# Two modulation tiles move from around the second branch's values to the end of attention

## The chip, the core and the metric

The kernel runs on one core of one Trainium2 chip. The metric is the device time of one execution in microseconds (us). Names in the text: TensorE is PE in the profile (its weight loads are PEld), VectorE is DVE, ScalarE is ACT, GpSimd is POOL, SyncE is SP. A line such as L203 is a line of the kernel before.

## What is computed

One decoder layer over 512 tokens of 1024 channels, in float32. A conditioning vector `c` gives six modulation vectors; two attention branches share one input projection; a gated MLP follows.

```python
mod = c @ w_ada + b_ada
sh1, sc1, gt1, sh2, sc2, gt2 = [m[:, None, :] for m in jnp.split(mod, N_MOD, axis=-1)]
u = x * (1.0 + sc1) + sh1
proj = u @ w_in
q_a, k_a, v_a, f_a, q_b, k_b, v_b, g_a, g_b = jnp.split(proj, _split_points(), axis=-1)
...
merged = jax.nn.sigmoid(g_a) * (y_fox @ w_fox_proj) + jax.nn.sigmoid(g_b) * (y_sb @ w_sb_proj)
attn_out = merged @ w_o
x = _layer_norm(DEEPNORM_ALPHA * x + (1.0 + gt1) * attn_out, ln1_g, ln1_b)
u2 = x * (1.0 + sc2) + sh2
```

Branch A is forgetting attention (softmax with a decay, "FoX"), branch B is stick-breaking attention. `sh2` and `sc2`, two of the six modulation vectors, are needed only after the first layer norm.

## The kernel before

**Products.** Every float32 weight is split into a rounded high half and the rest (`wh` by ScalarE at L183, `wl` by VectorE at L93), and each product is three matmuls, high by high, high by low and low by high (L134 to L136 for projections, L456 to L458 for the values).

**Items.** Weights come as tiles of 128x1024 (512 KB) through one list, `items`, in the order in which the code adds them. SyncE issues the loads in that order (L157). While attention runs, `depth` is 4: the load of an item is issued only after VectorE has read the item four places ahead of it (`paced`). The buffer `raw` has five slots, `wh` and `wl` three each. A projection that begins processes its own item and the two behind it.

**The stream.** The attention stage interleaves a list of TensorE work, `stream`, with the heads. The list holds the projections of queries and keys by pair of heads ("q4" is the tile of pair 4's queries; pairs 1 to 3 are of the stick-breaking branch, 4 to 7 of FoX), the values of a branch (`add_values`, four items, `vgroup`), the gates (`add_gate`) and the projections of the heads' outputs (`bproj`, whose weights are `in_wp`). `FILL` says how many matmuls stand between the steps of a head: scores (`stage_a`, L481 and L482), transposes of the probabilities (`stage_b`, L540), product with the values (`stage_c`, L558). PSUM has eight banks, given out in turn; a transpose needs three.

**Modulation tiles.** The 24 tiles of `in_wa` numbered 0 to 23 are items too. `add_ada` puts the next one into the list behind a projection. Numbers 8 to 23 are summed on VectorE against `c` by `mod_sum` (L203, one pass over 128x1024 with an accumulator, then DVE_READ_ACCUMULATOR) and feed `modr`, which L850 reads once all are there; they give `sh2` and `sc2`. Of the 27 places at which `add_ada` is called, 24 are used, in order; what is not placed by then is added behind the last projection.

**Order on the engines.** SyncE's order is that of the code. On the other engines a scheduler decides it when the kernel is built. The values of FoX are evacuated by `v_evac`: per bank two high halves on ScalarE (L90, `vv`) and two low halves on VectorE (L93, `vv`).

Of the kernel before, what the change touches and what calls it, by code (L numbers as in the profile page):

```python
# [51 lines left out]
def layer_kernel(ctx: ExitStack, tc: tile.TileContext, out, xT, x, cT, crow, wa0, wa1, bcol, bgt, w1, wct, wv, bf,  # L52
# [89 lines left out]
    def add_item(src, proc, cols=1024):  # L142
        items.append([src, proc, cols, None, None])
        return len(items) - 1
# [49 lines left out]
    for e in range(2):  # L194
        c = slice(e * 512, (e + 1) * 512)
# [383 lines left out]
    def ada_proc(n):  # L579
        def f(r):  # L580
            if 8 <= n < 24:
                mod_sum(2 + (n - 8) // 8, n % 8, r, slice(0, D), 0)
                return
            g, q = n // 4, n % 4
            if q == 0:
                ada_st[g] = z(F32, "ac2")
                V.tensor_scalar_mul(ada_st[g], r[:, 0:512], cTs[:, 0:1])  # L587
            acc = ada_st[g]
            for e in range(2):
                k = 2 * q + e  # L590
                if k > 0:
                    a = V.scalar_tensor_tensor(acc, r[:, e * 512 : (e + 1) * 512], cTs[:, k : k + 1], acc, ALU.mult, ALU.add)
                    state["read"] = a
        return f
# [24 lines left out]
    def gate_after(br, j):  # L619
        def f(ps):  # L620
            sg[(br, j)] = z(F32, "sg")
            S.activation(sg[(br, j)], ps, AF.Sigmoid)
        return f
# [42 lines left out]
    skip = [0]  # L666

    def add_ada(n=1):
        for _ in range(n):
            if skip[0]:  # L670
                skip[0] -= 1
            elif adas[0] < 24:
                add_item(wa1[adas[0]], ada_proc(adas[0]))
                adas[0] += 1
                if adas[0] in (4, 8):
                    stream.append((ada_split, (adas[0] // 4 - 1, len(items) - 1)))
                    sums.append([len(stream) + 3, adas[0] // 4 - 1])
# [4 lines left out]
    def add_proj(n, after):  # L682
        stream.append((proj, (add_item(wct[TILES.index(n)], split_proc), after)))
        flush_sum(len(stream))
# [12 lines left out]
    def add_pair(p):  # L697
        br, pr = seq[p]
        for c, ev in (("q", q_evac), ("k", k_evac)):
            if (c, p) in TILES:  # L700
                add_proj((c, p), lambda ps, ev=ev: ev(br, pr, ps))
                marks[(p, c)] = len(stream)
                add_ada(p > 1)

    def add_values(br, ada):
        for j in range(4):
            late = br == 0 and j == 2
            n = add_item(wv[br, j], v_proc if late else split_proc)
            if late:
                vfi.append(n)  # L710
            stream.append((vgroup, (br, j, n)))
            add_ada(ada)

    def add_gate(br, j):
        add_proj(("sb" if br == 1 else "fox", j), gate_after(br, j))
        add_ada()

    gb = list(range(NG, KT))
    add_pair(1)
    add_values(1, 1)  # L720
    marks["v1"] = len(stream)
    add_pair(2)
    add_gate(1, gb.pop(0))
    add_pair(3)
    add_gate(1, gb.pop(0))
    add_pair(4)
    marks["vf"] = len(stream) + 2
    add_values(0, 0)
    add_gate(1, gb.pop(0))
    add_pair(5)  # L730
    marks["y1"] = len(stream)
# [260 lines left out]
    for n in range(2 * FT):  # L992
        wui.append(add_item(wup[n], split_proc))
        if n in GTILES:
            k = GTILES.index(n)
            wai[(10, 28)[k // 4]] = add_item(wa1[(28, 24)[k // 4] + k % 4], ada_proc((28, 24)[k // 4] + k % 4))
        if n in (15, 19):
            p = (15, 19).index(n)
# [8 lines left out]
        if n in (28, 31, 32, 35):  # L1007
            k = (28, 31, 32, 35).index(n)
# [364 lines left out]
```

## Time and profile before

| | |
|---|---|
| median of 3 runs | 746.93 us (746.73 to 747.04) |
| the profiled execution's own time | 746.97 us |
| its span | 745.2 us |
| busy share of the span | PE 98%, PEld 82%, DVE 82%, ACT 52%, POOL 11% |
| the chain that ended last, by engine | PE 96%, DVE 2%, DMA 1%, ACT 1% |
| granted TensorE clock | 0.997 |

The span runs from the first instruction to the last of one execution; the run's own time is 1.8 us more. Of matmuls the end is modelled, so small gaps between them are read from their starts. "idle before <-X" in a timeline row is how long the engine stood ahead of that row, and what released it.

### The profile page before, as it was taken

How to read it: one execution, taken by the hardware profiler on the slowest of the kernel's cores; microseconds unless marked ns; L12 is line 12 of the kernel's file. 1: busy time of each engine (PE TensorE's matmuls, PEld its weight loads, DVE VectorE, ACT ScalarE, POOL GpSimd, SP SyncE). 2: the span in 40 equal slices, each digit the busy share in tenths (PEclk: the TensorE clock that was granted, in tenths of full speed). 3: DMA queues.
4: the chain of work that ended last, by engine and by line, in shares of the span. 5: the costliest groups of instructions: out<-in, count | busy, mean ns of one | idle time of the engine just before them, and what ended most of it. 6: DMA issues, size and time to landing. Idle time of an engine off the chain costs nothing.

```text
span 745.2 us, 9875 instructions
## 1 busy us (share of the span) xinstructions
PE 733.0 (98%) x3476; PEld 609.2 (82%) x3476; DVE 607.8 (82%) x1019; ACT 389.6 (52%) x683; POOL 83.0 (11%) x130
## 2 busy tenths in 40 slices
PE   8999999999999999999999999999999999999995
PEld 5878888887888888888889888888888888888885
DVE  6869799888788795884577899988877797779995
ACT  4566475694875654443055455444454453347550
POOL 1026223354000000000000000000001001000010
PEclk9999999999999999999999999999999999999998
DMA  9943545413413240652052788578788867647633
GB/s 324 404 177 113 170 170 181 158 58 114 171 58 114 72 155 28 211 191 84 1 211 87 206 289 241 201 214 247 246 303 226 252 198 216 211 156 227 223 88 85
DMA packets 45220, 131.95 MB, mean 177 GB/s; under 512 B 5905, under 2 KB 6417, under 8 KB 45170
## 3 DMA queue, kind: packets, MB, share of 16 engines
q1 hardware_dynamic: 38610, 113.66, 44.6%
q0 software_dynamic: 3536, 9.24, 6.6%
q10 hardware_dynamic: 3024, 8.41, 3.1%
q8 instruction: 27, 0.44, 0.2%
q14 instruction: 23, 0.19, 0.1%
HBM read 118.38 MB, written 12.85 MB: 176 GB/s over the span
## 4 chain that ended last, share of the span: by engine, by line
PE 96%; DVE 2%; DMA 1%; ACT 1%; issue 0%; DVEq 0%
PE ps L134 19%; PE ps L135 19%; PE ps L136 19%; PE ps L307 5%; PE ps L1102 5%; PE ps L1104 5%; PE ps L1103 5%; PE ps L558 3%; PE ps L540 2%; PE ps L900 2%; PE ps L899 2%; PE ps L901 2%; PE ps L457 2%; PE ps L458 2%; PE ps L456 2%; PE ps L481 1%
## 5 line engine op out<-in xcount | busy, mean ns | idle before, releaser
L183 ACT ACTIVATE wh<-raw 128x1024 fp32r<-128x1024 f32 (+1 forms) x105 | 109.4, 1044 | 111.0 <-PE ps L135 44.2
L93 DVE TENSOR_TENSOR wl<-raw,wh 128x1024 fp32r<-128x1024 f32 (+2 forms) x114 | 135.2, 1187 | 33.8 <-ACT wh L183 33.3
L134 PE MATMUL ps<-u2h,wh 128*128 128x512 f32 (+1 forms) x376 | 141.5, 376 | 0.0
L135 PE MATMUL ps<-u2l,wh 128*128 128x512 f32 (+1 forms) x376 | 141.2, 376 | 0.0
L136 PE MATMUL ps<-u2h,wl 128*128 128x512 f32 (+1 forms) x376 | 141.2, 376 | 0.0
L134 PEld LDWEIGHTS ps<-u2h,wh 128*128 128x128 f32 x376 | 70.8, 188 | 13.1 <-issue 0.3
L135 PEld LDWEIGHTS ps<-u2l,wh 128*128 128x128 f32 x376 | 70.8, 188 | 12.8
L136 PEld LDWEIGHTS ps<-u2h,wl 128*128 128x128 f32 x376 | 70.8, 188 | 12.7
L134 PE MATMUL ps<-uh,wh 128*128 128x512 f32 x200 | 79.4, 397 | 0.0
L135 PE MATMUL ps<-ul,wh 128*128 128x512 f32 x200 | 78.3, 391 | 0.0
L136 PE MATMUL ps<-uh,wl 128*128 128x512 f32 x200 | 78.2, 391 | 0.0
L1152 ACT ACTIVATE cv<-ps,cw 128x512 f32<-128x512 f32 x44 | 34.0, 773 | 43.8 <-PE ps L136 37.7
L1153 DVE SCALAR_TENSOR_TENSOR cv<-ps,cw,cv 128x511 f32<-128x511 f32 x44 | 32.8, 745 | 17.2 <-ACT cv L1152 17.1
L136 PEld LDWEIGHTS ps<-uh,wl 128*128 128x128 f32 x200 | 37.6, 188 | 8.2
L520 POOL TENSOR_TENSOR pt<-pt,om 128x127 f32<-128x127 f32 (+3 forms) x32 | 43.1, 1357 | 7.8 <-DVE om L519 7.8
L134 PEld LDWEIGHTS ps<-uh,wh 128*128 128x128 f32 x200 | 37.6, 188 | 7.3
L135 PEld LDWEIGHTS ps<-ul,wh 128*128 128x128 f32 x200 | 37.6, 188 | 7.2
L162 POOL DMA_DIRECT2D raw<-in_wdp x10 | 9.1, 909 | 248.6 <-DVE ac L587 184.2
L1154 DVE SCALAR_TENSOR_TENSOR cv<-ps,cw,cv 128x510 f32<-128x510 f32 x44 | 32.7, 742 | 0.3
L1160 ACT ACTIVATE cv<-cv 128x512 f32<-128x512 f32 x22 | 13.9, 630 | 33.4 <-DVE cv L1154 33.4
L519 DVE TENSOR_TENSOR_SCAN om<-om,dg 128x127 f32<-128x127 f32 (+3 forms) x32 | 29.6, 981 | 0.5 <-ACT om L514 0.5
L1104 PE MATMUL ps<-wh,hv 128*128 128x512 f32 x72 | 28.0, 389 | 0.0
(235 smaller groups left out, 1583.0 us busy)
## 6 DMA issues: line engine op xcount, KB each, us to landing
raw<-in_wup SPq DMA_DIRECT2D x44, 512.0 KB, 5.7
raw<-in_wa SPq DMA_DIRECT2D x32, 512.0 KB, 4.2
raw<-in_wct SPq DMA_DIRECT2D x25, 512.0 KB, 3.5
raw<-in_wdp SPq DMA_DIRECT2D x20, 512.0 KB, 6.0
wa<-in_wa SPq DMA_DIRECT2D x14, 512.0 KB, 8.3
raw<-in_wdp SPq DMA_DIRECT2D x22, 256.0 KB, 4.5
raw<-t SPq DMA_DIRECT2D x22, 256.0 KB, 3.9
raw<-in_wdp POOLq DMA_DIRECT2D x10, 512.0 KB, 7.8
```

The costliest lines, as they stand in the source:

```text
L93: state["read"] = V.tensor_tensor(o, i, fl(hi), ALU.subtract)
L134: PE.matmul(ps, wh, ah, start=first, stop=False)
L135: PE.matmul(ps, wh, al, start=False, stop=False)
L136: return PE.matmul(ps, wl, ah, start=False, stop=last)
L183: state["hi"] = S.activation(h[:, 0:cols], r[:, 0:cols], AF.Copy)
L307: PE.matmul(grp[g], w, u, start=j == 0 and n == 0, stop=j == KT - 1 and n == (1 if g == 7 else 2))
L520: G.tensor_tensor(pt[b][:, s : e - 1], pt[b][:, s : e - 1], om[:, s + 1 : e], ALU.mult)
L1102: PE.matmul(ps, ah, bh, start=first, stop=False, skip_group_check=onto)
L1103: PE.matmul(ps, ah, bl, start=False, stop=False, skip_group_check=onto)
L1104: return PE.matmul(ps, al, bh, start=False, stop=last, skip_group_check=onto)
L1152: S.activation(t, ps, AF.Identity, bias=cw[:, n, 3:4], scale=cw[:, n, 2:3])
L1153: V.scalar_tensor_tensor(t[:, 1:], ps[:, 0:511], cw[:, n, 1:2], t[:, 1:], ALU.mult, ALU.add)
```

## The change

```diff
@@ add_pair
             if (c, p) in TILES:
                 add_proj((c, p), lambda ps, ev=ev: ev(br, pr, ps))
                 marks[(p, c)] = len(stream)
-                add_ada(p > 1)
+                add_ada(p > 1 and (p, c) != (4, "k"))
@@
     add_pair(4)
     marks["vf"] = len(stream) + 2
     add_values(0, 0)
+    skip[0] = 1
     add_gate(1, gb.pop(0))
     add_pair(5)
```

`skip` stands in the kernel before as well, always 0: while it is above 0, a call of `add_ada` adds nothing and counts it down. So two places at which a tile was added, behind the keys of pair 4 (tile 11) and behind the gate that follows the FoX values (tile 12), stay empty. Each later tile comes two places later: 11 behind q5, 12 behind k5, 13 behind q6, 14 behind k6, and so on. The last two, 22 and 23, come behind the gates 5 and 6 of FoX, at two places that were not used. No operation is added or removed. SyncE issues as many loads, two of them later.

**VectorE at the evacuation of the FoX values.** `vv` are the values, `yf` and `yl` a finished head, `raw` with `modr` a modulation tile, `wl` a weight's low half, L503 the first softmax. Before:

```order
L203 SCALAR_TENSOR_TENSOR raw_1972,modr<-raw_1972,cbc 128x1024
L565 TENSOR_TENSOR yf_1672<-ps_1799,ytmp_1808 64x512
L93 TENSOR_TENSOR yl_1812<-yf_1672,yh_1811 128x512
L93 TENSOR_TENSOR vv_1818<-ps_1600,vv_1818 128x2x128
L93 TENSOR_TENSOR vv_1821<-ps_1600,vv_1821 128x2x128
L93 TENSOR_TENSOR vv_1830<-ps_1601,vv_1830 128x2x128
L203 SCALAR_TENSOR_TENSOR raw_2061,modr<-raw_2061,cbc 128x1024
L93 TENSOR_TENSOR vv_1833<-ps_1601,vv_1833 128x2x128
L93 TENSOR_TENSOR vv_1842<-ps_1602,vv_1842 128x2x128
L503 TENSOR_REDUCE sm_1888<-ps_1870 128x1
L503 TENSOR_REDUCE sm_1888<-ps_1872 128x1
L93 TENSOR_TENSOR vv_1845<-ps_1602,vv_1845 128x2x128
```

and after the change:

```order
L203 SCALAR_TENSOR_TENSOR raw_1967,modr<-raw_1967,cbc 128x1024
L93 TENSOR_TENSOR wl_1793<-raw_1737,wh_1792 128x1024
L565 TENSOR_TENSOR yf_1669<-ps_1799,ytmp_1808 64x512
L93 TENSOR_TENSOR yl_1812<-yf_1669,yh_1811 128x512
L93 TENSOR_TENSOR vv_1818<-ps_1603,vv_1818 128x2x128
L93 TENSOR_TENSOR vv_1821<-ps_1603,vv_1821 128x2x128
L93 TENSOR_TENSOR vv_1830<-ps_1604,vv_1830 128x2x128
L93 TENSOR_TENSOR vv_1833<-ps_1604,vv_1833 128x2x128
L93 TENSOR_TENSOR vv_1842<-ps_1605,vv_1842 128x2x128
L503 TENSOR_REDUCE sm_1888<-ps_1870 128x1
L503 TENSOR_REDUCE sm_1888<-ps_1872 128x1
L93 TENSOR_TENSOR vv_1845<-ps_1605,vv_1845 128x2x128
```

The tile between the third and the fourth `vv` is gone from there, and the tile ahead of `yf` (now number 12, before 14) stands ahead of the split of q5. Further up, the tile ahead of the last four stick-breaking scans (number 13 before) is gone too.

**VectorE ahead of the second FoX head's softmax.** `wl_2065` and `wl_2059` are q6, `wl_2146` and `wl_2140` are k6. Before:

```order
L93 TENSOR_TENSOR wl_2065<-raw_2059,wh_2064 128x1024
L203 SCALAR_TENSOR_TENSOR raw_2142,modr<-raw_2142,cbc 128x1024
L565 TENSOR_TENSOR yf_1994<-ps_1985,ytmp_1995 64x512
L93 TENSOR_TENSOR wl_2146<-raw_2140,wh_2145 128x1024
L503 TENSOR_REDUCE sm_2034<-ps_2016 128x1
```

and after, with `wl_1970` the split of k5, which stood between the softmax's reductions before:

```order
L93 TENSOR_TENSOR wl_1970<-raw_1914,wh_1969 128x1024
L93 TENSOR_TENSOR wl_2059<-raw_2053,wh_2058 128x1024
L565 TENSOR_TENSOR yf_1988<-ps_1979,ytmp_1989 64x512
L203 SCALAR_TENSOR_TENSOR raw_2136,modr<-raw_2136,cbc 128x1024
L93 TENSOR_TENSOR wl_2140<-raw_2134,wh_2139 128x1024
L503 TENSOR_REDUCE sm_2028<-ps_2010 128x1
```

The tile now stands directly ahead of k6's split, and k5's split has come down to this place. On TensorE, whose order is the same but for this, the second L481 of the third FoX head's scores now stands ahead of the first L482.

**VectorE and SyncE at the end of attention.** On VectorE before, with `wl_3177` gate 5, `wl_3213` gate 6, `raw_3125` and `raw_3165` the tiles 2 and 3 of `in_wo`:

```order
L93 TENSOR_TENSOR wl_3177<-raw_3163,wh_3176 128x1024
L639 TENSOR_TENSOR raw_3165<-raw_3165,gt_1207 128x1024
L93 TENSOR_TENSOR wol_3170<-raw_3125,woh_3168 128x512
L93 TENSOR_TENSOR wl_3213<-raw_3199,wh_3212 128x1024
L93 TENSOR_TENSOR wol_3171<-raw_3125,woh_3169 128x512
```

and after (`wl_3171` gate 5, `raw_3159` modulation tile 22, `raw_3193` and `raw_3119` tiles 3 and 2 of `in_wo`):

```order
L93 TENSOR_TENSOR wl_3171<-raw_3157,wh_3170 128x1024
L203 SCALAR_TENSOR_TENSOR raw_3159,modr<-raw_3159,cbc 128x1024
L639 TENSOR_TENSOR raw_3193<-raw_3193,gt_1207 128x1024
L93 TENSOR_TENSOR wol_3164<-raw_3119,woh_3162 128x512
L633 TENSOR_TENSOR sg_3000<-ps_3156,sg_3000 128x512
L93 TENSOR_TENSOR wol_3165<-raw_3119,woh_3163 128x512
```

Tile 22 stands between gate 5 and `in_wo` 3, and gate 6's split is no longer among these rows. The loads on SyncE from gate 5 on, after the change (`raw_3195` is gate 6, four places behind `in_wo` 2, which stands just ahead of these rows; `raw_3253` is tile 23):

```order
L157 DMA raw_3157<-in_wct 128x1024
L157 DMA raw_3159<-in_wa 128x1024
L157 DMA raw_3193<-in_wo 128x1024
L157 DMA raw_3195<-in_wct 128x1024
L157 DMA raw_3253<-in_wa 128x1024
L157 DMA raw_3255<-in_wp 128x1024
```

Before, no `in_wa` stood among them, and gate 6 was the second load behind gate 5.

## Prediction

> **What bounds the kernel now.** First the page's totals:
>
> ```profile
> span 745.2 us, 9875 instructions
> PE 733.0 (98%) x3476; PEld 609.2 (82%) x3476; DVE 607.8 (82%) x1019; ACT 389.6 (52%) x683; POOL 83.0 (11%) x130
> ```
>
> TensorE sets the time; the change takes no matmul away, so it can only change the time in which TensorE stands. Next the waits of TensorE alone, of which this is the longest inside attention:
>
> ```profile
> PE ps L540 <- DVE vv L93: 1.2, 2, 0.7
> ```
>
> It is the transposes of a head, which wait for PSUM banks that VectorE empties of FoX's values. The timeline of TensorE shows an undisturbed group of ten transposes and then this one:
>
> ```profile
> 167.97 1.25 PE L540 MATMUL ps<-ident,pt 128*128 128x128 f32 x10
> 168.98 0.48 PE L456 MATMUL ps<-wh,uh 128*128 128x512 f32 x1
> ...
> 183.71 0.60 PE L540 MATMUL ps<-ident,pt 128*128 128x128 f32 x4
> ...
> 186.27 0.48 PE L134 MATMUL ps<-uh,wh 128*128 128x512 f32 x1
> ```
>
> From the first transpose to the next matmul it is 1.01 there and 2.56 here: 1.55 us stand. The chain that ended last says what filled them:
>
> ```profile
> 173.57 4.50 DMA raw<-in_wa
> 178.16 1.23 DVE raw L203 x2
> 179.43 0.71 DVE yf L565
> 180.15 0.64 ACT yh L90
> 180.82 0.69 DVE yl L93
> 181.54 0.44 DVE vv L93
> 182.00 0.39 ACT vv L90
> 182.41 0.76 DVE vv L93 x2
> 183.17 1.14 DVE raw L203 x2
> 184.31 0.67 DVE vv L93 x2
> 184.97 0.53 DVE sm L503 x2
> 185.50 0.36 DVE vv L93
> ```
>
> VectorE works in order. It stood for the load of a modulation tile (14), summed it, and only then came to the head and to the values; a second tile (15) lay between the values. Both are the rows L203.
>
> **What the change removes.** Two sums leave the stretch ahead of the values, and all that follow stand for a later tile. Two things of before's VectorE timeline go with them:
>
> ```profile
> 151.67 1.82 DVE L203 SCALAR_TENSOR_TENSOR raw<-raw,cbc 128x1024 f32<-128x1024 f32 x1
> 156.21 1.39 DVE L93 TENSOR_TENSOR m<-ps,m 64x512 fp32r<-64x512 f32 x2
> 165.34 0.60 ACT L514 ACTIVATE om<-ps 128x512 f32<-128x512 f32 x1
> 166.70 1.22 DVE L203 SCALAR_TENSOR_TENSOR raw<-raw,cbc 128x1024 f32<-128x1024 f32 x1 [2.29 <-DMA raw<-in_wa]
> 167.85 3.75 DVE L519 TENSOR_TENSOR_SCAN om<-om,dg 128x127 f32<-128x127 f32 x4
> 174.57 1.21 DVE L93 TENSOR_TENSOR wl<-raw,wh 128x1024 fp32r<-128x1024 f32 x1
> ```
>
> *The scans.* They started at 167.85, behind tile 13, whose load was late. Without it they start with their input from ScalarE (the row of 165.34, which ends at 165.94; 0.17 earlier for the small gain below), take 3.75, and gate 7's split behind them, 1.2 as the row of 174.57, ends at 170.7. That read releases the load of tile 12; alone, it lands 3.3 later (the median of first loads, below), 174.0. Its sum and q5's split (1.25 each), then `yf`, `yh` and `yl` (0.7 each with the turns between VectorE and ScalarE) follow: the values begin at 178.6 and not at 181.54. Their six rows took from 181.54 to 185.86, with a sum of 1.14 among them; without it 3.2, and 0.4 for a turn of ScalarE that the sum covered, so 3.6 to 3.7: the last bank is free at 182.3. The transposes begin at 183.71 and want it later. The 1.55 go, with over 1.4 to spare, so they don't hang on the details.
>
> *A small one.* A product with values starts at 157.74, 0.32 behind the matmul before it where neighbours stand 0.23 apart, just after `m` (row 156.21) ended at 157.60. The sum of 151.67 is ahead of it; without it `m` ends near 155.9. I take 0.15: the 0.1, and half as much again for the restart.
>
> Gain: 1.55 + 0.15 = 1.7 us.
>
> **What it adds: a wait behind the values.** k5's split moves from the first softmax's reductions to behind the transposes' copies. The last of these copies and, further down, what follows:
>
> ```profile
> 191.95 0.55 DVE L93 TENSOR_TENSOR pl<-ps,ph 128x384 fp32r<-128x384 f32 x1
> ```
>
> From the last `vv` of the chain above to its end VectorE took 6.6 (185.86 to 192.50), with k5's split and without the sum that now takes its place, of like cost: so 182.3 + 6.6 = 188.9, and k5's split ends at 190.1. Only that read lets SyncE issue k6's load, with tile 14's behind it at 190.5. How long loads take:
>
> ```profile
> raw<-in_wct SPq DMA_DIRECT2D x20, 512.0 KB, 3.3
> raw<-in_wa SPq DMA_DIRECT2D x18, 512.0 KB, 4.3
> 198.58 0.42 SPq L157 DMA_DIRECT2D raw<-in_wa  x1
> 203.26 1.23 DVE L203 SCALAR_TENSOR_TENSOR raw<-raw,cbc 128x1024 f32<-128x1024 f32 x1 [1.07 <-DMA raw<-in_wa]
> 208.64 1.40 DVE L93 TENSOR_TENSOR m<-ps,m 64x512 fp32r<-64x512 f32 x2
> 209.68 0.28 PE L482 MATMUL ps<-m,s 68*128 68x256 f32 x1
> ```
>
> The `in_wct` loads are mostly first of a pair, the `in_wa` ones second. Tile 14 then lands at 194.8, while VectorE is through with q6's split and `yf` by 192.0 (190.1 + 1.2 + 0.7) and stands for it; k6's split is queued behind it. Sum 194.8 to 196.1, split to 197.3. That read releases the next pair (q7's load, then tile 15's at 197.7), and by the row of 198.58 such a tile is summed 4.7 after its issue: 202.4. Queued behind it are the query and key halves of pair 5, on which the third FoX head's scores wait. Before, `m` was done 6.07 after that sum began (203.26 to 209.33), 0.35 ahead of its user, the L482 of 209.68. Now it is done at 208.5. The L482 wants it at 209.68 - 1.7 + 0.1 (one more L481 ahead of it) = 208.1. So TensorE stands 0.4, and 0.1 for the way from VectorE's end to TensorE's start (157.60 to 157.74): 0.5.
>
> Ends: had tile 14 landed 3.9 after its issue, the wait would be 0.1; at 5.6, as the third load of a burst took (299.17 to 304.75, below), 1.8. I take 0.5, since tile 14 is second and the median of such is 4.3. The next head's scores use the same pair's keys.
>
> **The end of attention.** Two sums of 1.2 and two loads come in. That VectorE is later with the last pieces of `in_wo` is covered: the output projection begins with five of eight (`CUT`), for 60 matmuls, 13.6 us at 0.227. The order of the loads isn't covered as well: gate 6's load now waits for the last `wol` of `in_wo` 2, four places ahead.
>
> ```profile
> 298.26 0.33 SPq L157 DMA_DIRECT2D raw<-in_wct  x1
> 298.64 0.43 SPq L157 DMA_DIRECT2D raw<-in_wa  x1
> 299.17 0.37 SPq L157 DMA_DIRECT2D raw<-in_wp  x1
> 301.57 1.06 ACT L183 ACTIVATE wh<-raw 128x1024 fp32r<-128x1024 f32 x1
> 304.75 1.06 ACT L183 ACTIVATE wh<-raw 128x1024 fp32r<-128x1024 f32 x1 [1.53 <-DMA raw<-in_wp]
> 311.15 1.22 DVE L639 TENSOR_TENSOR raw<-raw,gt 128x1024 f32<-128x1024 f32 x1
> 314.08 0.69 DVE L93 TENSOR_TENSOR wol<-raw,woh 128x512 fp32r<-128x512 f32 x1
> 321.92 0.39 PE L136 MATMUL ps<-uh,wl 128*128 128x512 f32 x1
> ```
>
> On before's axis (TensorE and VectorE shift alike here): tile 22 takes 311.15, `in_wo` 3 comes 1.25 later, gate 6's split no longer stands between the two `wol`; the last ends at 315.4, not at 314.8. Gate 6's load goes out then, first of three, as gate 4's at 298.26 did; that one was on ScalarE 3.3 later. So 318.8, `wh` to 319.9, `wl` to 321.1. The L136 that needs it starts at 321.92, its weight load some 0.2 before: 0.6 to spare, cost 0. Gate 7's load goes out at 321.1, is there 4.3 later and split near 327.9; its projection begins 36 matmuls behind gate 6's, at 329.6. Ends: 0, and the second rival.
>
> [...]
>
> **The sum.** 1.7 - 0.5 = 1.2 us. Against the profiled execution's 746.97 (1.8 beyond its span) that is 745.8; against the median, 0.04 lower, 745.7. What a measurement of this kernel tells from no change is 0.2%, 1.5 us: so "the same", on the fast side.
>
> **Rivals.** *No new wait (25%).* If tile 14 or 15 lands a little earlier, or the copies end sooner, the scores aren't late and the whole 1.7 stays: 745.2, faster by 0.23%. For it: a half microsecond hangs on a chain of ten steps.
>
> *Gate 6 late (12%), the slower side.* If the three loads at 315.4 share the engines so that gate 6's takes what the third took, 5.5, its `wl` is done at 323.3: TensorE stands 1.6, and gate 7's load, released by that read, may add 0.3. With the wait at the scores as forecast: 745.7 + 1.9 = 747.6; with its upper end 748.8. It decides from a load of 5.1 (0.6 to spare and 1.2 to lose). Against it, the row 301.57.
>
> *The sums were not the cause (8%).* If ScalarE's turns or a bank's order hold the values, the wait stays and nothing changes: 746.9. The chain's rows speak against it.
>
> **Numbers.** The forecast, 55%, spans 745.3 to 747.0 by the ends of the new wait. Faster by over 0.2%: no new wait, 0.25, and 0.05 of the forecast's low end: 0.30. Slower by over 0.2%: half of gate 6 late, 0.06, and 0.04 for a wait that no row shows: 0.10. The same: 0.60. The range reaches from just under the first rival to the forecast's upper end, 745.0 to 747.0; outside it lies gate 6 late.
>
> **What would show it.** Right: no L540 row waits for `vv`, the values begin near 178.6, an L203 row near 194.8 with an idle of some 2.5 for its load, and an L482 near 208 that waits for `m`. Wrong: a gap at the L540 of 183.7; no gap at that L482; a gap at the first L136 of gate 6, near 320; or a new gap elsewhere, since TensorE's starts are otherwise the same to 0.1.

## The result and the profile after

The changed kernel takes 748.21 us in the median of 12 runs (746.12 to 750.17), the kernel before 746.96 in the 12 runs taken beside it. The ratio is 1.0016, 95% interval 1.0008 to 1.0023: 0.16% slower, where 0.16% faster was forecast, and above the range of 745.0 to 747.0. The profiled execution took 747.48. Measured twice more (e1 and e11 below) the changed kernel took 747.07 and 747.18, both at a ratio of 1.0000; one of e1's 11 executions took 1908.65 us, which leaves its median at 747.07 (747.04 without it), and is not counted further down.

The page's totals, and the waits of TensorE:

```profile
span 745.7 us, 9870 instructions
PE 733.1 (98%) x3476; PEld 609.8 (82%) x3476; DVE 608.5 (82%) x1019; ACT 389.4 (52%) x683; POOL 81.6 (11%) x130
...
PE ps L482 <- DVE m L93: 1.6, 1, 1.6
```

The wait of L540 for `vv` is gone from the list and a wait of L482 for `m` stands in its place. TensorE's timeline at the two places:

```profile
184.00 1.25 PE L540 MATMUL ps<-ident,pt 128*128 128x128 f32 x10
185.00 0.48 PE L134 MATMUL ps<-uh,wh 128*128 128x512 f32 x1
...
208.30 0.40 PE L481 MATMUL ps<-m,s 128*128 128x256 f32 x2
210.29 0.38 PE L482 MATMUL ps<-m,s 68*128 68x256 f32 x1 [1.59 <-DVE m L93]
```

The ten transposes take 1.00 again from the first to the next matmul, where they took 2.56: the 1.55 us of the forecast came. From the first L481 to the L482 it is 1.99 where two starts of this size take 0.22 (0.11 for one, by e8's rows 207.83 and 207.94 further down): 1.77 us stand, not 0.5. A start of the program that happened to be 0.44 later lies ahead of all this, so 0.44 is taken off wherever a time of after is held against one of the forecast. On balance this one execution lost 1.77, gained 1.55 and the small one, 0.15 (the 0.44 has shrunk to 0.29 at the first transpose, 184.00 for 183.71), and is level with before to 0.1 but for its start.

VectorE's timeline of after follows that chain:

```profile
166.25 3.14 DVE L519 TENSOR_TENSOR_SCAN om<-om,dg 128x127 f32<-128x127 f32 x4 [1.39 <-ACT om L514]
169.31 2.83 DVE L93 TENSOR_TENSOR wl<-raw,wh 128x1024 fp32r<-128x1024 f32 x1
...
175.40 1.22 DVE L203 SCALAR_TENSOR_TENSOR raw<-raw,cbc 128x1024 f32<-128x1024 f32 x1 [1.73 <-DMA raw<-in_wa]
...
179.92 0.42 DVE L93 TENSOR_TENSOR vv<-ps,vv 128x256 fp32r<-128x256 f32 x1
...
183.27 0.42 DVE L93 TENSOR_TENSOR vv<-ps,vv 128x256 fp32r<-128x256 f32 x1
...
190.27 2.35 DVE L93 TENSOR_TENSOR wl<-raw,wh 128x1024 fp32r<-128x1024 f32 x2
192.96 0.68 DVE L565 TENSOR_TENSOR yf<-ps,ytmp 64x512 f32<-64x512 f32 x1 [0.34 <-ACT ytmp L564]
196.67 1.23 DVE L203 SCALAR_TENSOR_TENSOR raw<-raw,cbc 128x1024 f32<-128x1024 f32 x1 [3.03 <-DMA raw<-in_wa]
...
204.19 1.23 DVE L203 SCALAR_TENSOR_TENSOR raw<-raw,cbc 128x1024 f32<-128x1024 f32 x1 [1.12 <-DMA raw<-in_wa]
...
209.56 1.40 DVE L93 TENSOR_TENSOR m<-ps,m 64x512 fp32r<-64x512 f32 x2
```

Every link is there: the values end at 183.7, tile 14's sum waits 3.03 for its load, tile 15's 1.12, `m` is late. From the values on all of it is 0.9 to 1.4 us later than forecast, and the row 169.31 is where that begins: gate 7's split took 2.83.

### The profile page after: what moved, and what is told of

It reads as the page before. It is cut to its first block, busy times and chain, and to the rows that moved or that the text cites. A ratio compares the mean times of both kernels' runs of the same rounds, so it can differ in the third digit from the quotient of the medians.

```text
span 745.7 us, 9870 instructions
## 1 busy us (share of the span) xinstructions
PE 733.1 (98%) x3476; PEld 609.8 (82%) x3476; DVE 608.5 (82%) x1019; ACT 389.4 (52%) x683; POOL 81.6 (11%) x130
## 4 chain that ended last, share of the span: by engine, by line
PE 92%; DVE 3%; DMA 2%; ACT 2%; issue 1%; DVEq 0%; SPq 0%; ACTq 0%
PE ps L135 18%; PE ps L134 18%; PE ps L136 18%; PE ps L307 5%; PE ps L1103 5%; PE ps L1104 5%; PE ps L1105 5%; PE ps L558 2%; PE ps L901 2%; PE ps L900 2%; PE ps L902 2%; PE ps L540 2%; DMA raw<-in_wa 2%; PE ps L457 1%; PE ps L458 1%; PE ps L456 1%
## 5 line engine op out<-in xcount | busy, mean ns | idle before, releaser
L93 DVE TENSOR_TENSOR wl<-raw,wh 128x1024 fp32r<-128x1024 f32 (+2 forms) x114 | 136.8, 1202 | 34.9 <-ACT wh L183 34.5
L136 PE MATMUL ps<-u2h,wl 128*128 128x512 f32 (+1 forms) x376 | 141.2, 375 | 0.0
L136 PEld LDWEIGHTS ps<-u2h,wl 128*128 128x128 f32 x376 | 70.8, 188 | 12.7
L136 PE MATMUL ps<-uh,wl 128*128 128x512 f32 x200 | 78.2, 391 | 0.0
L136 PEld LDWEIGHTS ps<-uh,wl 128*128 128x128 f32 x200 | 37.6, 188 | 8.3
```

The costliest lines, as they stand in the source:

```text
L93: state["read"] = V.tensor_tensor(o, i, fl(hi), ALU.subtract)
L136: return PE.matmul(ps, wl, ah, start=False, stop=last)
```

## Experiments

Two theories were set against each other first. The **scores theory**: what was lost is the wait of the scores for `m`. The **tail theory**: gate 6 is late at the end of attention in the longer executions. Later a third came in, the **clock theory**: a gap of TensorE in one piece can also lower the clock that the chip grants it (four of the changed kernel's first 12 executions are listed at 0.994 or 0.995, none of before's under 0.996).

**The changed kernel again, and three parts of it.**

*e1, the changed kernel once more.*

> The changed kernel once more, for a second profile and more times. Scores theory: what the change costs beyond its gain of 1.6 us is the wait of the third FoX head's L482 for m near 208, which was 1.9 us in the first profile and changes from run to run with the landing of tiles 14 and 15; median 747.5 to 748.7, this profile has a gap of 1 to 3.5 us there and none over 0.2 near 320. Tail theory: gate 6's projection is late in the slower runs; then the profile of a run over 748 has a gap at its first L136 near 320 and the gap at L482 stays at 1.9 or less.

Measured: 747.07 (ratio 1.0000, 0.9990 to 1.0009), below the expected 747.5. The gap at L482 was 1.33 and none stood near 320. So the 0.16% of the first measurement did not come again.

*e2, the last two tiles behind the last `in_wo`.*

```diff
+        if j + 3 == 5:
+            skip[0] = 3
         if j + 3 < KT:
             add_gate(0, j + 3)
-    skip[0] = 0
-    add_ada(24 - adas[0])
     while wos[0] < KT:
         add_wo()
+    skip[0] = 0
+    add_ada(24 - adas[0])
```

> Tiles 22 and 23 stand behind the last in_wo and not behind gates 5 and 6; up to there the lists are those of the changed kernel. Scores theory: as the changed kernel, 747.5 to 748.7 in the median and spread over 3 us or more, with the gap at L482 of 1 to 3.5. Tail theory: what the tail cost is gone, the median falls by 0.7 to 1.3 to 747.0 or below and the spread is that of before, 1.7 us.

Measured: 747.45 (1.0003, 0.9994 to 1.0012), spread over 2.2 us, with a gap of 1.86 at L482. Neither expectation is met in full, but emptying the tail brought nothing over e1: the tail theory falls.

*e3, the second edit alone, and e4, the first edit alone.*

```diff
# e3
-                add_ada(p > 1 and (p, c) != (4, "k"))
+                add_ada(p > 1)
# e4
-    skip[0] = 1
```

> Only the second edit: the place behind the gate stays empty, that behind the keys of pair 4 is used. VectorE's order from the last stick-breaking scans to m of pair 5 is that of the changed kernel; one tile is in the tail, behind gate 5. Scores theory: no gap at the L540 near 183.7, the gap at L482 of 1 to 3.5, median 747.5 to 748.7. Tail theory: with one tile there, gate 6's load is a place earlier, and the median is 746 to 747.

> Only the first edit: the place behind the keys of pair 4 stays empty, that behind the gate is used. VectorE's order at the values is that of before, with a sum ahead of yf and one between the values, and k5's split back among the softmax's reductions. Scores theory: the gap at the L540 near 183.7 is back (1.0 to 1.6 us), none over 0.3 at L482, median 746.6 to 747.3. Tail theory: the same within 0.3 unless one tile costs there as well. If the first edit alone cost time, it would be over 747.5.

The waits of TensorE, e3 and then e4:

```profile
PE ps L482 <- DVE m L93: 1.5, 1, 1.5
```

```profile
PE ps L540 <- DVE vv L93: 0.7, 1, 0.7
```

e3 took 747.51 (1.0009, 1.0000 to 1.0017) and has the changed kernel's gap at L482, 1.63 by the starts, and none at L540. e4 took 747.16 (1.0002, 0.9994 to 1.0011), has no gap at L482, and two of 0.23 and 0.85 among the transposes. e3 is just inside what was expected of it, and e4's gap of 1.08 in all too. So the swap of the one wait for the other is the work of the second edit alone.

**Why the wait was 1.8 and not 0.5.** Gate 7's split and GpSimd's products beside it, VectorE of before, GpSimd of before, GpSimd of after:

```profile
171.53 1.59 DVE L93 TENSOR_TENSOR wl<-raw,wh 128x1024 fp32r<-128x1024 f32 x1
```

```profile
170.53 1.51 POOL L520 TENSOR_TENSOR pt<-pt,om 128x255 f32<-128x255 f32 x1
```

```profile
168.54 1.88 POOL L520 TENSOR_TENSOR pt<-pt,om 128x127 f32<-128x127 f32 x2
170.37 0.09 POOL L516 MEMSET pt<- 128x1 f32 x1
170.43 0.63 POOL L520 TENSOR_TENSOR pt<-pt,om 128x255 f32<-128x255 f32 x1
```

In both kernels the split ends 1.08 after the 255-wide product: 173.12 behind 172.04, 172.14 behind 171.06. Its extra length looks like waiting. To test that, e5 takes those products away:

```diff
-                    G.tensor_tensor(pt[b][:, s : e - 1], ...)
+                    (br, h) == (1, 7) or G.tensor_tensor(pt[b][:, s : e - 1], ...)
```

> The changed kernel without GpSimd's products of the last stick-breaking head (L520), so the probabilities of that head are left as the sigmoid. Order elsewhere as in the changed kernel. Shared-path theory: gate 7's split at about 168.3 took 2.83 us because those products run beside it; now it takes 1.2, tile 12's load goes out 1.3 to 1.6 earlier, everything behind it too, and the gap at L482 near 208 falls from 1.3 to 1.9 to 0 to 0.6; median 0.8 to 1.4 below that of the changed kernel. Rival (the split waits for something else, ScalarE's half or the DMAs that GpSimd issues): it still takes over 2.3, and the gap stays over 1.

VectorE's timeline of e5:

```profile
165.28 2.96 DVE L519 TENSOR_TENSOR_SCAN om<-om,dg 128x127 f32<-128x127 f32 x4 [1.41 <-ACT om L514]
168.24 1.23 DVE L93 TENSOR_TENSOR wl<-raw,wh 128x1024 fp32r<-128x1024 f32 x1
```

The split takes 1.23 though GpSimd still issues its DMAs, everything behind it moves up, and the gap at L482 is gone. The median is 746.43 (0.9987, 0.9979 to 0.9996), 0.6 to 1.1 below the three kernels e1 to e3 with the gap; against the changed kernel itself (e1) it is 0.64, less than the 0.8 expected. That GpSimd's products hold up VectorE's split is shown: 2.83 with them, 1.23 without. That the products wait for VectorE in turn is only suggested: the 255-wide one took 1.51 beside the last scan before, and 0.63 after.

*e6, the two sums ahead of `m` taken out of the way.*

```diff
-                add_ada(p > 1 and (p, c) != (4, "k"))
+                add_ada(p > 1 and (p, c) not in ((4, "k"), (6, "k"), (7, "q")))
```

> The changed kernel with the places behind k6 and q7 empty too, so no sum stands on VectorE between the first FoX softmax and m of pair 5; the tiles come two more places later. Scores theory: the waits for tiles 14 and 15 were all of the gap; k6's split ends about 196.5, m is done near 206 to 207, no gap at L482, TensorE loses nothing from 183 to 212 but the usual 0.1 steps; 1.4 to 1.9 below the changed kernel unless the fuller tail takes some back (a gap between 310 and 350). Rival (the loads of the weights themselves are late): a gap of over 0.7 at L482 stays.

Measured: 745.99 (0.9977, 0.9968 to 0.9986), no wait of L482 left and no gap between 310 and 350, although the tail now holds four tiles more than before. Without the two sums and their loads there is no gap. The time fell by 1.08 against e1, less than the 1.4 to 1.9 expected, and about the 1.33 that e1's gap was long.

*e7 and e12, before without the place behind q6 only; e8, without those behind k5 and q6.*

```diff
# e7, e12
-                add_ada(p > 1)
+                add_ada(p > 1 and (p, c) != (6, "q"))
# e8
-                add_ada(p > 1)
+                add_ada(p > 1 and (p, c) not in ((5, "k"), (6, "q")))
```

> The kernel before with only the place behind q6 empty: the sum between the values is gone, the one ahead of yf stays. By the chain of before the last bank is free 0.7 earlier (1.14 less 0.4 for a turn of ScalarE), so the gap at the L540 of 183.7 falls from 1.55 to about 0.8, and no sum stands directly ahead of k6's split, so no gap at L482: 746.1 to 746.4. Rival (the sum that waits for its load sets the values alone): the gap stays over 1.3.

> The kernel before with the places behind k5 and q6 empty: no sum ahead of yf or among the first five values, and none directly ahead of k6's split; two tiles in the tail as in the changed kernel. Scores theory: both gaps are gone, the L540 of 183.7 and the L482 of 208: 745.2 to 745.6, 0.2% below before. Rival (with VectorE earlier, another wait comes up of the same size): a new gap of over 0.7 between 184 and 215, and 746.5 or more.

e7 missed on the other side: 748.97 (1.0022, 1.0012 to 1.0032). TensorE's waits and VectorE's timeline of e7:

```profile
PE ps L540 <- DVE vv L93: 2.2, 1, 2.2
```

```profile
183.68 0.76 DVE L93 TENSOR_TENSOR vv<-ps,vv 128x256 fp32r<-128x256 f32 x2 [0.31 <-ACT vv L90]
184.35 1.01 DVE L503 TENSOR_REDUCE sm<-ps 128x1 f32<-128x256 f32 x2
185.28 1.22 DVE L93 TENSOR_TENSOR wl<-raw,wh 128x1024 fp32r<-128x1024 f32 x1
186.41 0.42 DVE L93 TENSOR_TENSOR vv<-ps,vv 128x256 fp32r<-128x256 f32 x1
```

With the sum gone, the scheduler put reductions and k5's split ahead of the last of the six values: where two gaps of 0.65 and 0.85 stood before, there is one of 2.37.

e8 took 745.70 (0.9980, 0.9971 to 0.9989), 0.1 over the expected range, and is below both kernels. Its VectorE and TensorE:

```profile
177.57 0.42 DVE L93 TENSOR_TENSOR vv<-ps,vv 128x256 fp32r<-128x256 f32 x1
...
206.88 1.40 DVE L93 TENSOR_TENSOR m<-ps,m 64x512 fp32r<-64x512 f32 x2
```

```profile
207.83 0.28 PE L481 MATMUL ps<-m,s 128*128 128x256 f32 x1
207.94 0.28 PE L482 MATMUL ps<-m,s 68*128 68x256 f32 x1
```

The values begin 4 us earlier than before, `m` is ready 0.3 ahead of the scores, and neither gap is there. It also moves two tiles into the tail: so which two places are left empty decides whether anything is gained.

**The clock.** The longest execution of the changed kernel took 750.17, at a mean granted clock of 0.994; the longest of the kernel before, over all the runs, took 748.90, and none of its listed clocks is under 0.996. Sorted by the clock listed for each execution:

| kernels | longest gap inside attention as profiled, us | executions | at 0.995 or less | median of these | median of the rest |
|---|---|---|---|---|---|
| before (beside the experiments) | 0.85 | 108 | 0 | | 747.06 |
| e4, e6, e8, e9, e10 | up to 0.85 | 55 | 0 | | |
| changed kernel (first, e1, e11) | 1.33 to 1.77 | 33 | 7 | 748.37 | 747.10 |
| e2, e3 | 1.63, 1.86 | 22 | 3 | 748.50 | 747.45 |
| e7, e12 | 2.24, 2.37 | 22 | 9 | 749.16 | 748.09 |

The gap left out of the column is one of 0.7 near 55 that all kernels have. e5 is left out as well: its profiled execution is listed at 0.947 throughout, yet took 745.62, so a listed clock alone proves nothing. The mean is a coarse sign besides. The profiles of after and of before show half clock at the end, behind the last matmul, for 3.4 and 3.9 us, and that alone makes their means 0.998 and 0.997. By the same sum an execution like after's with one more stretch, 3.4 us at the 0.53 that e11 shows below, could still be listed at 0.996, so the table counts too few rather than too many. Before was run on the chips of e1 to e12 as well, so the chip is not the reason.

To make such a gap on purpose, e9 and e10 take e8 and write the keys' low half two and four times more:

```diff
-            state["k"] = lo_of(d["m2"][0:64, :], ps[r, :], d["m1"][0:64, :])
+            for _ in range(3 if (br, p, hh) == (0, 1, 0) else 1):   # e10: 5
+                state["k"] = lo_of(d["m2"][0:64, :], ps[r, :], d["m1"][0:64, :])
```

> The kernel without the places behind k5 and q6 (no gap between 183 and 215, 745.7), with the low half of the keys of pair 5's first head written two more times by VectorE (the same values), so that TensorE's L482 near 208 waits about 2.5 us in one piece. Plain theory (a gap costs its own length): 745.7 + 2.5 = 748.2, mean clock of the executions 0.996 to 0.998 as in the kernel without it. Clock theory (a gap of this length can also make the chip grant TensorE a lower clock for a while, in some executions): about a third to a half of the executions show a mean clock of 0.995 or less and are 1 to 2 us longer than the rest; median 748.2 to 749.5.

> The same with four more writes: one gap of about 5.1 us. Plain theory: 750.8, mean clock 0.996 or more. Clock theory: nearly all executions at 0.995 or less, 752 to 755, and in the profile a stretch of a few us behind the gap in which matmuls of 512 columns start further apart than 0.227.

Both failed to make a gap: 746.22 (0.9984, 0.9975 to 0.9993) and 745.65 (0.9978, 0.9970 to 0.9987), no clock under 0.996. TensorE's timeline of e10 (its L483 is the L482 of the others):

```profile
207.60 0.63 PE L482 MATMUL ps<-m,s 128*128 128x256 f32 x3
208.06 0.40 PE L134 MATMUL ps<-uh,wh 128*128 128x512 f32 x1
...
212.74 0.28 PE L483 MATMUL ps<-m,s 68*128 68x256 f32 x1
```

The scheduler knew of the longer work on VectorE and set projection matmuls in between. They don't test the clock theory; they only add executions without a gap, and without a low clock, to the table.

*e11, the changed kernel a third time.*

> The changed kernel a third time, on the chip of the other two. Clock theory: executions at 0.995 or less appear again (1 to 5 of 11) and are the longest; the rest lie at 746.5 to 748 like before. Plain theory: no tie between clock and time.

747.18 (1.0000, 0.9990 to 1.0010), two of 11 at 0.995, and the profiled execution is one of them (748.18). TensorE's timeline, then the busy time and granted clock (PEclk) by stretches:

```profile
209.26 0.38 PE L482 MATMUL ps<-m,s 68*128 68x256 f32 x1 [1.58 <-DVE m L93]
...
211.40 0.63 PE L135 MATMUL ps<-ul,wh 128*128 128x512 f32 x1
211.83 0.63 PE L136 MATMUL ps<-uh,wl 128*128 128x512 f32 x1
212.25 0.63 PE L134 MATMUL ps<-uh,wh 128*128 128x512 f32 x1
...
214.45 0.39 PE L134 MATMUL ps<-uh,wh 128*128 128x512 f32 x1
214.68 0.40 PE L135 MATMUL ps<-ul,wh 128*128 128x512 f32 x1
```

```profile
200.00:208.00 8.00, 7.68 (x37) 1.00 0.26 98
208.00:210.80 2.80, 1.53 (x10) 0.96 0.40 130
210.80:214.20 3.40, 3.40 (x11) 0.53 0.14 49
214.20:220.00 5.80, 5.80 (x33) 1.00 0.27 90
```

The gap of 1.75 is followed by 3.4 us at about half the clock: the matmuls start 0.43 apart and not 0.23, and seven of them lose 1.5 us together. A clock of 0.53 for 3.4 us takes 0.0021 off the mean of 745 us, which is the step from 0.997 to 0.995 of the table.

> The kernel with only the place behind q6 empty once more; its gap at the L540 near 184.5 was 2.4 us in one piece, the longest of all. Clock theory: again 4 to 7 of 11 executions at a mean clock of 0.995 or less, those the longest by 1 to 2 us; where the profiled execution is one of them, matmuls of 512 columns behind the gap start about 0.43 apart instead of 0.227 for some 3 us. Plain theory: 747.8 in the median, 0.9 over before by the longer gap, and no execution under 0.996.

e12: 748.83 (1.0020, 1.0010 to 1.0030), a gap of 2.24 in one piece, 4 of 11 executions at 0.995. The profiled one was not among them, so the low clock behind this gap was not seen in a trace. Nor were the four the longest, which had been expected: two at 0.996 took 749.15 and 749.20, longer than three of the four, and the medians are 0.6 apart where 1 to 2 was expected.

## Why the prediction was wrong, point by point

- **The wait at the values goes, 1.55, and the small one, 0.15.** Right: 1.55 and 0.15.
- **The values begin at 178.6 and end at 182.3.** Measured 179.5 and 183.25 (less 0.44). This is the step that failed first. "Gate 7's split behind them, 1.2 as the row of 174.57": the row of the same split, 171.53, says 1.59 beside GpSimd's products, and without the sum the split came earlier against those products and took 2.83. The place was found, the duration was taken from a row beside which none of GpSimd's products ran. The split was 1.6 too long, the scans ahead of it 0.6 shorter than the 3.75 taken, which leaves 1.0. For the first gap it did not matter, since over 1.4 was to spare; the second gap has nothing to spare, so it took the full microsecond.
- **A new wait at the L482, 0.5.** The mechanism and the place were right, the term mis-sized: 1.77. Of the 1.27 that were missed, about 1.0 came with gate 7's split (in e5, where it takes 1.23, there is no gap) and the rest with tile 14's load, 4.7 from issue to landing where 4.3 was taken. The upper end, 1.8, was right by its size, though not by its cause (a load of 5.6), and gives the 747.0 at which the range ended; the two repeats, 747.07 and 747.18, are what that sum forecasts.
- **The clock.** No case priced it: the forecast put it at nothing. Of the kernels with a gap of 1.3 to 1.9 in one piece, 10 of 55 executions show the lower clock; their medians are 1.0 to 1.3 us above the rest, and e11's rows lose 1.5. Before, the 1.5 stood in two pieces with transposes between, and none of 108 executions shows it. That the pieces make the difference is argued, not shown, since no run cut the same gap in two at the same place.
- **The tail, 0.** Right, but by luck: 0.6 was thought to be to spare, and nothing was. Gate 6's load went out at 316.50 (less 0.44: 316.06, where 315.4 was forecast), its split ends at 322.29, and the weight load of its first L136, due at 322.27 by the spacing of those ahead of it, starts at 322.34. The L136 itself still starts on time, at 322.50. e2 shows nothing to be had there. The rival "gate 6 late" did not come: gate 6's load was on ScalarE 3.47 after its issue (316.50 to 319.97), not 5.5.
- **"The sums were not the cause".** Refuted: the gap at L540 went with them. That is no rule for one sum alone: in e7, without the sum between the values, the gap came back larger, because the order had changed.
- **What stays open.** The changed kernel's first 12 executions have the median 748.21, the next 10 and 11 have 747.04 and 747.18. Of the first 12, four are at 0.995 or less; the other eight lie at 746.1 to 748.9, with a median of 747.68. Of the three of these above 748, two are listed at 0.996, where a stretch of half clock can't be excluded; before, too, has 16 of 108 above 748. Why the first measurement lay a microsecond over the two repeats no run shows. Over all 33 the median is 747.31, 0.3 over before.

## What to carry to other kernels

Where a removed stall lets an engine run ahead, take each duration behind it from a row with the same neighbours, since the neighbour may be what set it: gate 7's split took 1.59 and 2.83 beside GpSimd's products and 1.23 without them. Look at the pieces of a TensorE stall as well as at its sum: here two pieces of 0.65 and 0.85 cost their length (1.55 came when they went), and with a piece of 1.3 us or more 19 of 77 executions show a lower clock besides. And work that is moved out of one wait turns up at the next place of the same queue: the version that won (e8) has no sum between gate 7's split and the first five values, and none directly ahead of k6's split.

## What the hardware showed that was not expected

In e11's profile TensorE ran at a granted clock of 0.53 in 3.4 us close behind a gap of 1.75 us. Not every execution of such a kernel shows it: a mean of 0.995 or less stands in none of 163 executions of kernels with gaps up to 0.85, in 10 of 55 with 1.3 to 1.9, and in 9 of 22 with 2.2 to 2.4. The link of gap and clock rests on these counts and on one profile. In after's profile the clock stayed at 1.00 behind a gap of 1.77, in e7's behind one of 2.37. What decides which executions are hit, no run here shows.
